# The loads and splits of the weights carry the highest priority of the scheduler

## The chip, the core and the metric

The kernel runs on one core of a Trainium2 chip. The metric is the device time of one execution in microseconds (us); the time before is the median of three runs. A profiled execution is a further run, and what is read from the trace belongs to that one alone.

The engines have these names in the rows: PE is TensorE (matrix products; PEld its weight loads), DVE is VectorE, ACT is ScalarE, POOL is GpSimd, SP is SyncE, which here issues DMA transfers only. Each engine works through its own list of instructions.

## The reference

Two blocks in sequence, everything in float32. x and ctx are 256 x 2048 each.

```python
for l in range(2):                                   # first block
    shift, scale, gate = split(silu(c) @ w_ada[l] + b_ada[l], 3)         # and the same for c_ctx
    h  = rms(x, norm_w[l]) * (1 + scale) + shift     # hc from ctx in the same way
    qa, ka, va, qb, kb, vb, qc, kc, vc, z = project_stream(h, w_in[l], ...)
    o = three kinds of attention (8, 12 and 6 heads) on queries of h, keys of h and hc
    x = x + gate * ((o * silu(z)) @ w_out[l])        # and ctx, in the first layer only
h = rmsnorm(x, pre_norm_mix)                         # second block
x = x + rmsnorm(token_mixer(h, w_in_2, ...), ...)    # spatial gating and gated linear attention
x = x + rmsnorm(memory_cross_attention(...), ...)
x = x + rmsnorm(conv_ffn(rmsnorm(x, ...), ffn_w_up, ..., ffn_w_down), ...)
```

What takes the time are the dense products with large weights: w_in (2048 x 6208, twice), w_out, w_in_2 (2048 x 12304), the projections of the mixer, and the feed-forward weights (2048 x 11264 and 5632 x 2048).

## The kernel before

**Products.** A float32 product is made of three products in a faster format, float32r. Each operand is split into hi (the value rounded to float32r) and lo (the rest), and the kernel adds hi by hi, hi by lo and lo by hi. `split` (L418) does this with one copy on ACT (L420) and one subtraction on DVE (L421). Activations are split once and kept; weights are split as they stream in.

**The weight stream.** `order()` lists all pairs of weight tiles (two times 128 x up to 512 values, 512 KB) in the order of their use, 894 pairs in all. `load` (L441) takes a buffer of the tag raw, of which there are three, and issues the transfer on SP (L448). `run_ahead` (L451) takes one tile of a loaded pair, a buffer each of the tags hi and lo (four of each), and splits. `weights` (L433) hands a pair to a product. In the text of the program a split stands about two tiles ahead of its use.

**Dense loops.** `dense` (L462) has activations as stationary operand and adds up one PSUM bank for each column group of 128 tokens: four groups for most products of the first block, two elsewhere. `denseT` (L488) has weights as the stationary operand. Both use the tag d, of which there are four banks. After the last k-tile the caller's evac empties the banks on ACT, DVE or both.

**Everything else.** Norms, attention and gates are cut into small stages (`push`, `urge`, `defer`) that `tick` (L368) calls between matrix products, by a clock of estimated TensorE time. So the text of the program already interleaves dense work with attention.

**adaLN.** For the first layer, `ada_pe` (L668) computes shift and scale on PE, from 256 KB loads on SP (L689, L694), in five parts; each part of h is usable when its part is there. The other shifts, scales and gates come from `ada_steps` (L718): loads on SP (L736) and a product with a running sum on DVE (L739), strewn over the first block.

**What sets the order.** The kernel is written for a scheduler that receives all instructions in one block, each with a priority that is its place in the text. It goes through the block with a model of the engines' times. Whenever an engine is free in that model, it takes, among the instructions whose inputs and buffers are there, the one of the lowest number. The order that comes out is fixed for each engine, with semaphores where one engine needs another. On the chip every engine keeps to that order, whatever the real times are.

**The start.** `block1` (L1408) issues the sixteen loads of x and ctx (L1441) in turn with the sixteen first adaLN loads (L689), squares and sums each row of tokens on ACT (L515), and makes h through transposes, DVE (L540) and ACT (L543). The first products (`first_products`, L1382) need h.

Of the kernel before, what the change touches and what calls it, by code (L numbers as in the profile page):

```python
# [235 lines left out]
class K:  # L236
# [204 lines left out]
    def load(self):  # L441

        if self.order_at < len(self.order):
            name, k0, pieces = self.order[self.order_at]
            self.order_at += 1
            raw = self.str.tile([128, 2, 512], F32, name=self.name("raw"), tag="raw", bufs=3)
            n, src = self.w(name).block(k0, pieces)
            self.nc.sync.dma_start(raw[:, :, :n], src)  # L448
            self.loaded += [raw[:, j, :n] for j in range(2)]

    def run_ahead(self):  # L451

        if not self.loaded:
            self.load()
        if self.loaded and len(self.whole) < 2:
            raw = self.loaded.pop(0)
            n = raw.shape[-1]
            hi, lo = (self.str.tile([128, 512], F32R, name=self.name(x), tag=x, bufs=4) for x in ("hi", "lo"))
            self.split(hi[:, :n], lo[:, :n], raw)
            self.whole.append((hi, lo))  # L460

    def dense(self, act, kts, w, pieces, cols, evac, what="d", skip={}):  # L462
# [177 lines left out]
class Block1(K):  # L640
# [266 lines left out]
    def layer(self, l, h, hl, hcols, qcols, x_get, x_put):  # L907
# [161 lines left out]
        def job_ab(g, m, s):  # L1069
# [56 lines left out]
            for hd in (2 * m, 2 * m + 1):  # L1126
                for q in range(2):
                    st = [lambda hd=hd, q=q: load(hd, q), self.ahead] if g == "a" and s == 0 else []
                    st += [lambda hd=hd, q=q: prepare(hd, q), self.padding, lambda hd=hd, q=q: first(hd, q), self.soft, lambda hd=hd, q=q: part(hd, q), self.lag, lambda hd=hd, q=q: second(hd, q)]
                    self.push(*st, *([self.lag2, end] if hd % 2 and q else []))  # L1130
# [886 lines left out]
```

## Time and profile before

| | us |
|---|---|
| median of three runs | 3467.62 (3465.45 to 3474.96) |
| profiled execution | 3477.03 |
| its span, from first to last instruction | 3475.3 |
| TensorE busy in the span | 3353.6 |
| VectorE busy | 2298.3 |
| ScalarE busy | 1788.2 |
| mean granted TensorE clock | 0.985 of 2.4 GHz |

A row of a timeline has the start and the length in us, the engine, the line of the program, the operation, what is written and read, and how many instructions were merged; in brackets stands the idle time of the engine just before, and what ended it. A row of a list of waits has the engine and line that waited, what ended the wait, the total in us, how many times, and the longest. A row of stretches has, for each engine, busy time and instructions, then the granted clock (1.00 is 2.4 GHz, 0.50 is 1.2 GHz), the busy share of the DMA engines and GB/s.

### The profile page before, as it was taken

What the parts mean: (1) busy time and instruction counts of PE and PEld (TensorE: products, weight loads), DVE (VectorE), ACT (ScalarE), POOL (GpSimd) and SP (SyncE); (2) the same over time, 40 slices, a digit from 0 to 9 for tenths busy, and PEclk for the clock granted to TensorE, in tenths of its full rate; (3) what the DMA queues carried; (4) which work ended last, traced back from release to release, by engine and by line L of the source; (5) the groups of instructions that cost most, each with busy time, mean ns of one, the idle gap of its engine ahead of it and who ended that gap; (6) DMA issues with size and microseconds to landing.
All of it is one profiled execution on the core that took longest, in us unless ns stands there. A gap on an engine that the chain in (4) does not pass through costs nothing. (4 is left out here: it accounts for less than half of the span.)

```text
span 3475.3 us, 54483 instructions
## 1 busy us (share of the span) xinstructions
PE 3353.6 (96%) x19530; PEld 2879.6 (83%) x19530; DVE 2298.3 (66%) x4939; ACT 1788.2 (51%) x3556; POOL 315.7 (9%) x472
## 2 busy tenths in 40 slices
PE   7999999999999999999999999999999899999998
PEld 4577778788787888887777999888788899999886
DVE  3488988778866576887664555555666766666554
ACT  3345655346435365765474445545556555555544
POOL 0022210103120121111200000000000000000000
PEclk9999999999999999999999999999999999999999
DMA  8845444642565544444544535555655455555554
GB/s 295 290 118 153 130 146 144 207 131 86 172 210 158 162 113 139 143 153 139 176 145 158 183 116 182 192 190 190 205 177 168 146 182 183 182 187 196 189 194 164
DMA packets 226767, 590.28 MB, mean 170 GB/s; under 512 B 39904, under 2 KB 63184, under 8 KB 226496
## 3 DMA queue, kind: packets, MB, share of 16 engines
q1 hardware_dynamic: 221104, 570.41, 51.1%
q0 software_dynamic: 4864, 15.69, 1.5%
q8 instruction: 153, 2.51, 0.3%
q14 instruction: 118, 0.97, 0.1%
q10 hardware_dynamic: 528, 0.71, 0.1%
HBM read 582.48 MB, written 4.24 MB: 169 GB/s over the span
## 5 line engine op out<-in xcount | busy, mean ns | idle before, releaser
L421 DVE TENSOR_TENSOR lo<-raw,hi 128x512 fp32r<-128x512 f32 (+3 forms) x1788 | 1206.7, 679 | 846.2 <-ACT hi L420 838.7
L420 ACT ACTIVATE hi<-raw 128x512 fp32r<-128x512 f32 (+3 forms) x1788 | 1090.4, 614 | 1238.0 <-DVE lo L421 271.1
L502 PE MATMUL upd<-hi,hi 128*128 128x256 f32 x1408 | 399.2, 284 | 0.0
L504 PE MATMUL upd<-lo,hi 128*128 128x256 f32 x1408 | 399.1, 283 | 0.0
L505 PE MATMUL upd<-hi,lo 128*128 128x256 f32 x1408 | 398.8, 283 | 0.0
L739 DVE SCALAR_TENSOR_TENSOR scr<-raw,cb 128x512 f32<-128x512 f32 x448 | 299.1, 693 | 35.8 <-DMA raw<-in_w_ada_dram 17.8
L504 PEld LDWEIGHTS upd<-lo,hi 128*128 128x128 f32 x1408 | 270.8, 192 | 0.3 <-DVE lo L546 0.3
L505 PEld LDWEIGHTS upd<-hi,lo 128*128 128x128 f32 x1408 | 270.8, 192 | 0.0
L502 PEld LDWEIGHTS upd<-hi,hi 128*128 128x128 f32 x1408 | 270.7, 192 | 0.0
L399 POOL TENSOR_TENSOR sm<-sm,mhalf 128x2 f32<-128x2 f32 (+4 forms) x116 | 117.0, 1010 | 1406.2 <-DVE sm L398 1400.9
L481 PE MATMUL downd<-hi,hi 128*128 128x512 f32 x352 | 137.7, 391 | 0.0
L483 PE MATMUL downd<-hi,lo 128*128 128x512 f32 x352 | 137.7, 391 | 0.0
L482 PE MATMUL downd<-lo,hi 128*128 128x512 f32 x352 | 137.6, 391 | 0.0
L602 ACT ACTIVATE P<-Ss,sm 128x512 f32<-128x512 f32 (+1 forms) x164 | 99.5, 608 | 67.7 <-DVE sm L598 49.6
L408 ACT ACTIVATE PT<-pTt 128x256 f32<-128x256 f32 x226 | 79.3, 381 | 64.9 <-PE pTt L619 55.0
L481 PE MATMUL L0outd<-hi,hi 128*128 128x512 f32 x256 | 101.2, 395 | 4.3 <-DVE ot L1361 3.0
L505 PE MATMUL L0zd<-hi,lo 128*128 128x512 f32 x256 | 100.4, 392 | 2.4 <-DVE lo L421 2.4
L598 DVE TENSOR_REDUCE sm<-Ss 128x1 f32<-128x512 f32 (+1 forms) x164 | 95.1, 585 | 8.9 <-PE Ss L591 7.9
L502 PE MATMUL L0zd<-hi,hi 128*128 128x512 f32 x256 | 100.4, 392 | 0.4 <-DVE kpe L414 0.4
L482 PE MATMUL L0outd<-lo,hi 128*128 128x512 f32 x256 | 100.1, 391 | 0.0
L483 PE MATMUL L0outd<-hi,lo 128*128 128x512 f32 x256 | 99.8, 392 | 0.3 <-DVE lo L421 0.3
L504 PE MATMUL L0zd<-lo,hi 128*128 128x512 f32 x256 | 100.0, 391 | 0.0
(570 smaller groups left out, 8451.3 us busy)
## 6 DMA issues: line engine op xcount, KB each, us to landing
raw<-in_w_in_dram SPq DMA_DIRECT2D x344, 512.0 KB, 3.6
raw<-in_w_ada_dram SPq DMA_DIRECT2D x384, 256.0 KB, 3.5
raw<-in_ffn_w_up_dram SPq DMA_DIRECT2D x176, 512.0 KB, 3.3
raw<-in_w_out_dram SPq DMA_DIRECT2D x104, 512.0 KB, 3.6
raw<-in_ffn_w_down_dram SPq DMA_DIRECT2D x88, 512.0 KB, 3.2
raw<-in_w_proj_b_dram SPq DMA_DIRECT2D x32, 512.0 KB, 3.3
raw<-in_w_in_dram SPq DMA_DIRECT2D x32, 288.0 KB, 3.3
raw<-in_w_proj_a_dram SPq DMA_DIRECT2D x16, 512.0 KB, 4.0
```

Of the source, the lines that this page charges most:

```text
L399: nc.gpsimd.tensor_tensor(r, ms, self.mhalf[:, :n], op=OP.pow)
L420: self.nc.scalar.activation(hi, src, AF.Copy)
L421: self.nc.vector.tensor_sub(lo, src, hi.bitcast(F32))
L481: nc.tensor.matmul(ps[t][:, a], lhsT=xh, rhs=hi[:, a], start=first, stop=False)
L482: nc.tensor.matmul(ps[t][:, a], lhsT=xh, rhs=lo[:, a], start=False, stop=False)
L483: nc.tensor.matmul(ps[t][:, a], lhsT=xl, rhs=hi[:, a], start=False, stop=last)
L502: nc.tensor.matmul(p, lhsT=hi[:, s], rhs=xh, start=kt == 0 and c % per == 0, stop=False, skip_group_check=True)
L504: nc.tensor.matmul(p, lhsT=hi[:, s], rhs=xl, start=False, stop=False, skip_group_check=True)
L505: nc.tensor.matmul(p, lhsT=lo[:, s], rhs=xh, start=False, stop=kt == nk - 1, skip_group_check=True)
L598: nc.vector.tensor_reduce(nm[:, 0:1], S[:, :nk], op=OP.max, axis=AX.X, negate=True)
L602: nc.scalar.activation(P[:, :nk], S[:, :nk], AF.Exp, bias=nm[:, 0:1], accum_out=nm[:, 1:2])
L739: nc.vector.scalar_tensor_tensor(self.temp("scr"), raw, 1.0, st[s], op0=OP.mult, op1=OP.mult, accum_out=st["p"][:, s, k, q:q + 1])
```

## The change

The issue of each weight load, and both instructions of each weight split, are written inside `high_priority()`. This context gives what is written in it the priority numbers from zero on, as if it stood at the start of the program, and goes back to the former count on its exit. No instruction is added, removed or changed in shape, and the numbers of buffers stay as they are. Splits of activations (`halves`, `unit`) keep their priority.

```diff
@@ -445,7 +445,8 @@
             self.order_at += 1
             raw = self.str.tile([128, 2, 512], F32, name=self.name("raw"), tag="raw", bufs=3)
             n, src = self.w(name).block(k0, pieces)
-            self.nc.sync.dma_start(raw[:, :, :n], src)
+            with self.tc.high_priority():
+                self.nc.sync.dma_start(raw[:, :, :n], src)
             self.loaded += [raw[:, j, :n] for j in range(2)]
 
     def run_ahead(self):
@@ -456,7 +457,8 @@
             raw = self.loaded.pop(0)
             n = raw.shape[-1]
             hi, lo = (self.str.tile([128, 512], F32R, name=self.name(x), tag=x, bufs=4) for x in ("hi", "lo"))
-            self.split(hi[:, :n], lo[:, :n], raw)
+            with self.tc.high_priority():
+                self.split(hi[:, :n], lo[:, :n], raw)
             self.whole.append((hi, lo))
```

## Rows read from the trace of the kernel before

**Rows 1.** The page's first part: busy time, share of the span, instructions.
```profile
PE 3353.6 (96%) x19530; PEld 2879.6 (83%) x19530; DVE 2298.3 (66%) x4939; ACT 1788.2 (51%) x3556; POOL 315.7 (9%) x472
```

**Rows 2.** Stretches: the start up to the first product, and the up projection.
```profile
0.00:36.00 36.00, 16.10 (x91) 6.87 (x91) 7.09 (x37) 16.46 (x43) 8.68 (x31) 1.00 0.97 345
2708.00:3219.00 511.00, 511.00 (x4247) 510.70 (x4246) 339.75 (x582) 286.35 (x486) 2.18 (x4) 1.00 0.55 182
```

**Rows 3.** Waits of PE: on splits of weights, and one on an eviction.
```profile
PE L1qbd L481 <- ACT hi L420: 5.1, 1, 5.1
PE mbd L481 <- ACT hi L420: 3.1, 1, 3.1
PE xkd L505 <- DVE lo L421: 3.1, 1, 3.1
PE vsd L481 <- ACT hi L420: 2.9, 2, 2.6
...
PE L0zd L505 <- DVE lo L421: 2.4, 3, 1.3
...
PE L0cqd L482 <- DVE lo L421: 2.2, 1, 2.2
...
PE L1qbd L482 <- DVE lo L421: 1.8, 4, 1.1
...
PE L0vbd L481 <- DVE a L1403: 1.6, 3, 0.9
```

**Rows 4.** Stretches behind five waits, PE alone: busy (x), clock, DMA, GB/s.
```profile
499.90:503.30 3.40, 3.40 (x12) 0.50 0.82 242
1356.40:1363.50 7.10, 5.95 (x17) 0.50 0.43 142
1769.60:1773.00 3.40, 3.37 (x15) 0.51 0.57 167
2452.50:2455.70 3.20, 3.20 (x7) 0.50 0.59 205
2592.30:2595.70 3.40, 3.40 (x18) 0.50 0.72 224
```

**Rows 5.** Timeline of the start, up to the first dense product.
```profile
1.35 0.70 POOL L775 DMA_DIRECT2D rows<-in_rows_dram  x1 [0.34 <-issue]
...
24.44 1.01 SPq L448 DMA_DIRECT2D raw<-in_w_in_dram  x2
...
27.21 0.63 ACT L515 ACTIVATE scr<-x 128x512 f32<-128x512 f32 x1 [1.31 <-DMA x<-in_ctx_dram]
...
35.94 0.78 PE L481 MATMUL L0firstd<-hi,hi 128*128 128x512 f32 x1
```

**Rows 6.** Timeline of DVE before the wait of L0cqd.
```profile
496.67 0.68 DVE L739 SCALAR_TENSOR_TENSOR scr<-raw,cb 128x512 f32<-128x512 f32 x1
...
497.88 1.28 DVE L421 TENSOR_TENSOR lo<-raw,hi 128x512 fp32r<-128x512 f32 x2
```

**Rows 7.** Timeline of DVE before the wait of xkd.
```profile
2586.34 4.77 DVE L1522 SCALAR_TENSOR_TENSOR x<-y,sm,x 128x512 f32<-128x512 f32 x4 [0.44 <-POOL sm L399]
```

**Rows 8.** Timeline of ACT before the wait of vsd.
```profile
1766.98 0.63 ACT L1591 ACTIVATE e<-e 128x512 f32<-128x512 f32 x1
```

**Rows 9.** Timeline of ACT in the product L1qbd.
```profile
1340.04 0.94 ACT L420 ACTIVATE hi<-raw 128x384 fp32r<-128x384 f32 x2 [2.08 <-DMA raw<-in_w_in_dram]
```

**Rows 10.** Timeline of ACT before the wait of mbd.
```profile
2451.19 0.63 ACT L515 ACTIVATE scr<-mem 128x512 f32<-128x512 f32 x1 [4.18 <-DMA mem<-in_mem_dram]
...
2451.82 0.61 ACT L420 ACTIVATE hi<-raw 128x512 fp32r<-128x512 f32 x1
```

**Rows 11.** Timeline of DVE where L0firstd ends and L0vbd begins.
```profile
219.55 0.68 DVE L421 TENSOR_TENSOR lo<-raw,hi 128x512 fp32r<-128x512 f32 x1
...
220.15 1.28 DVE L1403 TENSOR_TENSOR a<-a,L0firstd 128x512 f32<-128x512 f32 x2
```

**Rows 12.** Waits of ACT: its longest on slots of one product of layer 0.
```profile
ACT hi L420 <- PE L0zd L504: 98.4, 51, 2.7
```

## The prediction

> **What bounds the kernel now.** I read the page first: TensorE is busy for 3353.6 us of a span of 3475.3 us [rows 1]. So at most the remaining 122 us, and whatever TensorE does at a slow clock, can be won by any reordering. Next I cut the span into stretches: in the 511 us of the up projection, TensorE is busy for all 511 us [rows 2]. There the splits already keep up, and another order can win nothing. Third, I listed what TensorE waits for [rows 3]. The reader is to look for two names there: "ACT hi L420" and "DVE lo L421" are the two halves of a split, and a dense product (L481 to L483, L502 to L505) that waits for one of them lacks a weight. These rows add up to 5.1 + 3.1 + 3.1 + 2.9 + 2.4 + 2.2 + 1.8 = 20.6 us. Fourth, I asked for the granted clock just after the five longest of those waits [rows 4]. It stands at 0.50 (1.2 GHz) for 3.4, 7.1, 3.4, 3.2 and 3.4 us, where it is 2.4 GHz in steady work. Half of each such stretch is lost: 1.7 + 3.5 + 1.7 + 1.6 + 1.7 = 10.2 us. A late split therefore costs 20.6 + 10.2 = 30.8 us in all, which is the whole prize of the change.
>
> **Does the scheduler do what the edit asks?** The trace shows that it hoists what is ready as far as it can: the load of "rows" belongs to rope_tables, which the code calls behind the whole first product, and yet GpSimd issues it at 1.35 us [rows 5]. An instruction at priority zero is therefore taken the moment that its buffer is free and its data is there. What stays the limit is buffers: three for raw, four each for hi and lo. No split can go further ahead than these allow, and the amount of work on every engine stays the same. Only orders change: of ACT and DVE (1788 splits on each), and of SP (894 loads).
>
> **Part 1, splits on DVE and ACT: a gain.** Before L0cqd's wait of 2.2 us, DVE runs adaLN products (L739), and only then two lo halves [rows 6]. What L739 makes is a gate that the output product is the first to use, so nothing is lost by taking the lo first. The same order makes L0zd wait (2.4 us), and before xkd's wait DVE does four steps of the residual update, 4.77 us, and then the lo [rows 7]. I take these three whole: 2.2 + 2.4 + 3.1 us of waits and 1.7 + 1.7 us of slow clock, 11.1 us. The wait of vsd (2.9 us, and 1.7 us of clock) has ACT busy with logarithms and exponentials (L1586, L1591) in front of a split [rows 8]: whole, 4.6 us. L1qbd (5.1 + 1.8 us, and 3.5 us of clock, 10.4 us) I take at two thirds, 6.9 us: in that stage ACT also waits for the raw load itself, 2.08 us at one place [rows 9], and no priority helps against that. mbd (3.1 us, and 1.6 us of clock, 4.7 us) I take at half, 2.4 us: there ACT stands at a Square that waits 4.18 us for the memory input, and the split behind it starts right when the Square ends [rows 10]. If the scheduler believes that the input has landed earlier than it does, it will again put the Square first. Sum: 11.1 + 4.6 + 6.9 + 2.4 = 25.0 us saved. The bounds are 11.1 us (only the DVE places) and 30.8 us (all of it).
>
> **Part 2, loads on SP: a loss at the start.** Before, the first raw load is issued at 24.44 us, behind all sixteen loads of x and ctx and the sixteen first adaLN loads on the same queue [rows 5]. At priority zero it is ready at time zero, since its buffers are empty. Three raw loads of 512 KB fill the three buffers. Their splits need only themselves, and two tiles of four halves go through at once (four slots), which frees two more raw buffers. So five loads, 5 x 524 KB = 2.62 MB, go ahead of nearly all of x. The start is bound by transfer: 345 GB/s and a DMA share of 0.97 in the first 36 us [rows 2], so five loads put the last x back by 2.62 MB / 345 GB/s = 7.6 us, and three by 4.6 us. All of it is on the path: the last Square of ctx starts at 27.21 us because it waited for its load, and the first dense product follows at 35.94 us through a chain of norm, adaLN and transposes that contains no weight [rows 5]. Nothing is paid back, as TensorE does not run short of weights later in that stage. I take 7.6 us lost, with bounds 4.6 and 7.6 us. A gain is excluded, since the first product waits for h and not for a weight. Later on the same queue the raw loads also pass adaLN loads, bias loads and gates. Each is put back by an issue of about half a us (two took 1.01 us [rows 5]), and all of them are asked for well ahead of their use by the text, so I take nothing for that; without that cover it would be half a us for each that PE waits for.
>
> **Part 3, what the splits push back: a loss at changes of product.** In layer 0 a product of four column groups fills all four banks that dense work has. The next product needs the last bank nine matmuls after the change, and nine of 512 columns at 2.4 GHz are 1.9 us. An eviction of about 0.7 us fits into that with one split of 0.68 us ahead of it, and with two it does not. The trace has one such place: at 219.55 us a lo half goes ahead of the additions that empty the banks, and TensorE then waits for "a L1403" three times [rows 11], 1.6 us in total [rows 3]. The code has 43 changes with all four banks in use (34 in layer 0, 9 in layer 1). In such stages a slot falls free only once in a k-tile of four column groups, so two ready splits are rare. I take one change in ten, 4 x 1.6 = 6.4 us lost, with bounds 0 and twice that, 12.8 us. In the second block a product uses two of the four banks, so an eviction has a whole product's time, and this costs nothing there. Attention's softmax steps are also pushed back, by at most the few splits that the slots allow, and dense work covers them on TensorE, so I take nothing; where no dense work is left, it would be 0.68 us for each such split.
>
> **Sum.** 25.0 us saved, 7.6 + 6.4 = 14.0 us lost: 11.0 us less. The profiled execution took 3477.0 us (span 3475.3 us and 1.7 us around it), 9.4 us above the median of 3467.6 us, so the forecast is 3466 us for such an execution and 3467.6 - 11.0 = 3456.6 us for the median; I write 3456. About 0.3% (10.4 us) is what a measurement of this kernel can tell from no change, and the forecast lies just past it. Its own range is 3441 (30.8 us saved, 4.6 us lost, no bank waited for) to 3477 (11.1 us saved, 7.6 + 12.8 us lost).
>
> **Rivals.** *The waits move on.* The wait for a split goes, but what was ahead of it is then late: k stacks behind L1qbd, exponentials behind vsd, and TensorE waits there instead. Half of the gain stays, 12.5 us, against 14.0 us lost: 1.5 us more, 3469 us. For it: TensorE's list has dozens of small waits of other kinds. Against it: most of them have dense work ready to fill the place.
>
> *Evictions held in the queue, slower.* The place is the change of product in layers 0 and 1, and the price is the 1.6 us of the one that the trace shows. ACT already stands at the head of its queue for a slot: 51 times, 98.4 us in all, for L0zd alone [rows 12]. A split put early then holds what is behind it. If 20 of the 43 changes pay, that is 32 us: 25.0 saved, 7.6 + 32 lost, 14.6 us more, 3482 us. It decides from about 11 changes on, where 17.4 us eat the net gain of 25.0 - 7.6. Against it: only one of the 43 shows the cost now, although lo halves stand among evictions in many places. The Trainium skill, "Perfetto Trace Analysis", section "Tensor Engine Instruction (MATMUL, LD_WEIGHTS)", says that the queues of ACT, DVE and GpSimd are strictly first in, first out, so an early split that isn't ready stops all behind it. By that rule this rival is the natural outcome. The trace agrees as far as the order goes: the ready split behind the waiting Square started only after it [rows 10].
>
> *The order hardly changes.* If splits are ready just when nothing else is, as in the second block, only the start moves: 7.6 us more, 3475 us. Against it: DVE's order before L0cqd shows a case where both were ready [rows 6].
>
> **Chances.** The forecast 0.44; the waits move on 0.27; evictions held 0.19; order unchanged 0.10. The second and the fourth lie within 0.3%. So faster 0.44, same 0.37, slower 0.19. For eight in ten I take 3440 to 3484: it holds the forecast's range, both middle cases and about half of the slow one.
>
> **What would show it.** Right: the first dense product starts at about 43 us; raw loads are SP's first issues; the rows of L0cqd, L0zd and xkd that wait for L421 are gone, and with them the half clock at 500 and 2592 us; the up projection takes 511 us still. Wrong: the first product starts where it did (loads not hoisted); waits for "a L1403", "ot L1361" or other evictions grow past 13 us; L1qbd waits for DMA instead; or new stretches of half clock behind attention's steps.

## The result, and the profile after

The kernel became slower. The median went from 3469.6 to 3503.7 us, a ratio of 1.0092 with a 95% interval of 1.0078 to 1.0105, about 32 us (the two medians as they stand are 34 us apart, the figure that the expectations use). The forecast was 3456 us, with 3440 to 3484 as its range; both the sign and the range were wrong. The profiled execution of the changed kernel took 3503.4 us, with a span of 3501.6 us against 3475.3 us: 26.3 us more. In the changed kernel's rows the lines of `dense` and `denseT` are two higher than before (L481 is now L483, L505 is L507), and up to two higher in the runs below; the split stays at L420 and L421.

The page's first part of the kernel after, the line that answers to [rows 1]:

```profile
PE 3365.2 (96%) x19530; PEld 2878.7 (82%) x19530; DVE 2304.3 (66%) x4939; ACT 1792.7 (51%) x3556; POOL 319.5 (9%) x472
```

The same instructions run, but TensorE is busy for 11.6 us more and idle for 14.7 us more (136.4 against 121.7 us). The next view is that of stretches, as in [rows 2]: the start and the up projection after.

```profile
0.00:47.00 47.00, 18.15 (x106) 7.18 (x107) 9.22 (x40) 18.37 (x46) 10.53 (x31) 1.00 0.92 308
2734.00:3245.00 511.00, 510.94 (x4240) 509.94 (x4239) 342.83 (x580) 288.83 (x485) 2.18 (x4) 1.00 0.54 182
```

The up projection is as it was. The start now takes 47 us instead of 36, and at a lower rate of transfer: 308 GB/s over the stretch instead of 345. The waits of TensorE after come first below, and the rows of the same kinds before in the second fence:

```profile
PE adao L700 <- DMA raw<-in_w_ada_dram: 29.6, 9, 19.2
...
PE sts L851 <- DVE kl L874: 5.0, 3, 3.5
PE trs L532 <- DVE sm L398: 3.6, 1, 3.6
...
PE Ss L593 <- DVE kl L872: 3.0, 3, 2.2
...
PE pTt L621 <- DVE P L614: 2.9, 5, 1.1
PE L0zd L507 <- DVE lo L421: 2.7, 1, 2.7
...
PE sts L851 <- POOL ro L806: 2.6, 2, 2.2
PE vsd L483 <- ACT hi L420: 2.6, 3, 0.9
PE L0vbd L483 <- DVE a L1405: 2.2, 3, 1.0
PE sts L851 <- DVE q L874: 1.8, 1, 1.8
...
PE mbd L483 <- ACT hi L420: 1.2, 1, 1.2
...
PE L1qbd L483 <- ACT hi L420: 0.4, 1, 0.4
...
PE xkd L507 <- DVE lo L421: 0.2, 1, 0.2
```

```profile
PE adao L698 <- DMA raw<-in_w_ada_dram: 13.0, 7, 8.9
...
PE trs L530 <- DVE sm L398: 2.4, 1, 2.4
...
PE sts L849 <- DVE kl L872: 2.3, 3, 1.5
...
PE Ss L591 <- DVE kl L870: 1.9, 1, 1.9
...
PE pTt L619 <- DVE P L612: 0.8, 2, 0.5
...
PE sts L847 <- DVE q L872: 0.2, 1, 0.2
```

Three things are to be seen. The change does what it says: the waits for splits of [rows 3] shrink from 20.6 us to about 8 us, and L0cqd's is gone. Against them stand longer or new ones, the largest of them on steps of attention and rope (kl, P, q, ro) and on one of a norm (sm). These six kinds grew by 2.7 + 1.1 + 2.1 + 1.6 + 2.6 + 1.2 = 11.3 us (ro has no row before); smaller kinds grew and shrank beside them. And the products of adaLN wait 16.6 us longer for their own loads.

Read along the groups of dense products, the loss comes in two parts. The first dense product starts 11.1 us later and L0vbd, the first group behind the first products, 17.4 us later (238.36 us instead of 220.98). Between there and the end another 9 us come, in many pieces, with gains in between that don't last.

### The profile page after: what moved, and what is told of

It is laid out like the page before. It is cut to its first block, busy times and chain, and to the rows that moved or that the text cites. A ratio compares the mean times of both kernels' runs of the same rounds, so it can differ in the third digit from the quotient of the medians.

```text
span 3501.6 us, 54518 instructions
## 1 busy us (share of the span) xinstructions
PE 3365.2 (96%) x19530; PEld 2878.7 (82%) x19530; DVE 2304.3 (66%) x4939; ACT 1792.7 (51%) x3556; POOL 319.5 (9%) x472
## 4 chain that ended last, share of the span: by engine, by line
PE 58%; issue 12%; DVE 6%; ACT 2%; DMA 1%; POOL 1%; POOLq 0%; DVEq 0%; ACTq 0%; SPq 0%
PE upd L506 5%; PE upd L507 5%; PE upd L504 5%; PE downd L485 2%; PE downd L483 2%; PE downd L484 2%; DVE lo L421 2%; PE L0outd L483 1%; PE oo L636 1%; PE L0outd L485 1%; PE L0outd L484 1%; PE Ss L593 1%; PE wo2d L484 1%; PE wo2d L483 1%; PE wo2d L485 1%
## 5 line engine op out<-in xcount | busy, mean ns | idle before, releaser
L421 DVE TENSOR_TENSOR lo<-raw,hi 128x512 fp32r<-128x512 f32 (+3 forms) x1788 | 1207.2, 679 | 856.5 <-ACT hi L420 845.4
L420 ACT ACTIVATE hi<-raw 128x512 fp32r<-128x512 f32 (+3 forms) x1788 | 1091.5, 614 | 1271.1 <-DVE lo L421 268.1
L507 PE MATMUL upd<-hi,lo 128*128 128x256 f32 x1408 | 398.9, 283 | 0.0
L507 PEld LDWEIGHTS upd<-hi,lo 128*128 128x128 f32 x1408 | 270.9, 192 | 0.0
L483 PE MATMUL downd<-hi,hi 128*128 128x512 f32 x352 | 137.7, 391 | 0.0
L483 PE MATMUL L0outd<-hi,hi 128*128 128x512 f32 x256 | 101.1, 395 | 4.3 <-DVE ot L1363 2.9
L507 PE MATMUL L0zd<-hi,lo 128*128 128x512 f32 x256 | 100.6, 394 | 2.7 <-DVE lo L421 2.7
```

The costliest lines, as they stand in the source:

```text
L420: self.nc.scalar.activation(hi, src, AF.Copy)
L421: self.nc.vector.tensor_sub(lo, src, hi.bitcast(F32))
L483: nc.tensor.matmul(ps[t][:, a], lhsT=xh, rhs=hi[:, a], start=first, stop=False)
L507: nc.tensor.matmul(p, lhsT=lo[:, s], rhs=xh, start=False, stop=kt == nk - 1, skip_group_check=True)
```

## The experiments

All ratios are to the kernel before, on the same chip, with 95% intervals; 0.1% is 3.5 us. In each diff the lines are those of `load` or `run_ahead`, and `order_at` is the number of the pair in the order of use. The first products use pairs 1 to 24, the rest of the first layer pairs 25 to 159, the second layer 160 to 318, and the second block 319 to 894.

### Loads against splits, early against late

```
e1_loads:   with self.tc.high_priority():                                   # load only
e2_splits:  with self.tc.high_priority():                                   # split only
e3_late:    with self.tc.high_priority() if self.order_at > 24 else ...     # load and split
e4_early:   with self.tc.high_priority() if self.order_at <= 24 else ...    # load and split
```

> Only the weight loads carry the priority; the splits keep their place in the text. Theory L (the loss is made on SP: raw loads stand ahead of x and of adaLN loads, at the start and in the first stage): first dense product at about 47 us as in the changed kernel, waits of adaLN products for their loads well above the 13 us of before, time 17 to 30 us above before. Theory Q (the loss is made in the queues of ACT and DVE, where splits stand ahead of other work): only the start costs, 8 to 11 us above before, and the rest of the loss of 34 us is gone.

> Only the splits carry the priority; the loads keep their place in the text. Theory L: the first dense product starts at about 36 us as before, the waits of L0cqd, L0zd and xkd for the lo half are gone, time 0 to 11 us below before. Theory Q: 15 to 25 us above before, with longer waits for evictions and attention's steps.

> Loads and splits carry the priority from the 25th pair of weight tiles on, that is behind the pairs of the first products. Theory L: start and first stage as before; what is left is the rest, which by the starts of the dense groups was about 9 us between 220 us and the end: 5 to 10 us above before. Theory Q: the 17 us of start and first stage are not all from there, and 15 to 25 us above before are left.

> Loads and splits carry the priority for the first 24 pairs alone, those of the first products. Theory L: L0vbd starts about 17 us later than before and nothing is paid back: 17 to 25 us above before, and together with the kernel that has the other pairs it adds up to the loss of the whole change, 34 us. Theory Q: 8 to 11 us above before, the start alone.

Measured: e1_loads 1.0045 (1.0031 to 1.0058), e2_splits 1.0049 (1.0036 to 1.0062), e3_late 1.0043 (1.0031 to 1.0056), e4_early 1.0046 (1.0031 to 1.0061). Each is about 15 us slower, and either pair adds up to the loss of the whole. So both theories hold, each for one half, though the loads alone stay just under theory L's 17 to 30 us. With the loads alone, the first dense product starts 11.0 us late and L0vbd 15.2 us late, and the rest of the kernel just follows: the last product starts 13.6 us late. With loads and splits raised from pair 25 on (e3_late), the first dense product starts as before and L0vbd 1.8 us late, and the loss collects from the second group of z to the end of the second layer. That the splits would cost nothing, as theory L had it, fell; so did theory Q's view that loads cost at the start only.

The two halves lose their time in different places. These are the first parts of the pages of e1_loads (span 3489.0 us) and e2_splits (span 3486.1 us):

```profile
PE 3351.7 (96%) x19530; PEld 2878.4 (82%) x19530; DVE 2300.5 (66%) x4939; ACT 1788.0 (51%) x3556; POOL 319.1 (9%) x472
PE 3365.1 (97%) x19530; PEld 2882.0 (83%) x19530; DVE 2304.0 (66%) x4939; ACT 1792.4 (51%) x3556; POOL 318.1 (9%) x472
```

With the loads alone TensorE is busy about as long as before (3353.6 us) and idle for 137.3 us instead of 121.7: that half is waiting. With the splits alone it is idle for 121.0 us, as before, and busy for 11.5 us more, at a mean granted clock of 0.987 (0.985 before). So the new waits only take the place of those that went, and what is lost is TensorE's own time for the same instructions. e3_late has most of its loss there too (3367.7 us busy, 125.4 us idle). Each profile is a single execution, but all ten in which no split behind pair 24 is raised lie between 3346.4 and 3360.3 us busy, and the changed kernel, e2_splits, e3_late, e13_lo and e14_off40 between 3361.5 and 3367.7 us.

### The start and the first stage

```
e5_three:   ... if self.order_at <= 3 else ...          # load and split
e10_five:   ... if self.order_at <= 5 else ...
e9_mid:     ... if 4 <= self.order_at <= 24 else ...
```

> Only the first three pairs carry the priority, so SP has three weight loads ahead of x and none that waits for a buffer. Theory T (the start is lost to transfer alone, bytes over 345 GB/s): the first dense product is 4.6 us later than before, the fourth and fifth load cost the other 3.0 us of five, and the 9.5 to 11 us of the runs with five need another reason. Theory S (SP stands at the fourth load until a buffer is free, with x behind it): three loads give 4 to 6 us and the rest of the 11, 5 to 7 us, is the standing; and the first stage behind it loses nothing, as its loads are where they were before. Time 4 to 7 us above before in both; 10 or more would say that the place of the first load, not the buffers, matters.

> Loads and splits of the first five pairs alone carry the priority. With three, the first dense product was 6.1 us later, and the first stage behind it 5.2 us shorter. Theory S: first dense product 9.5 to 11 us later than before, and since only three loads' worth of that is paid back, L0vbd 5 us later or more, time 5 to 10 us above before. Theory A: the first stage pays back all of it as with three, L0vbd within 2 us of before, time within 4 us of before, and the loss of 14 us of the first 24 pairs comes from pairs 6 to 24.

> Loads and splits of pairs 4 to 24 carry the priority; the first three stay behind x and the first adaLN loads. Theory A (in the first stage raw loads ahead of adaLN loads cost by themselves): the first dense product at 36 us as before, L0vbd 4 to 8 us later than before, time 4 to 8 us above before. Theory S (what costs is the fourth and fifth load at the start, where SP stands with x behind it): first dense product and L0vbd within 2 us of before, time within 3 us of before.

Measured: e5_three 1.0007 (0.9998 to 1.0017), e10_five 1.0007 (0.9998 to 1.0016), e9_mid 1.0020 (1.0009 to 1.0031). The rows are PE's timelines, the first dense product and the first of L0vbd, for e5_three, e10_five and e9_mid in this order:

```profile
42.07 0.48 PE L483 MATMUL L0firstd<-hi,hi 128*128 128x512 f32 x1
221.87 0.47 PE L483 MATMUL L0vbd<-hi,hi 128*128 128x512 f32 x1 [0.95 <-DVE a L1405]
```

```profile
46.42 0.78 PE L483 MATMUL L0firstd<-hi,hi 128*128 128x512 f32 x1
227.98 0.47 PE L483 MATMUL L0vbd<-hi,hi 128*128 128x512 f32 x1 [0.95 <-DVE a L1405]
```

```profile
36.72 0.78 PE L483 MATMUL L0firstd<-hi,hi 128*128 128x512 f32 x1
232.93 0.47 PE L483 MATMUL L0vbd<-hi,hi 128*128 128x512 f32 x1 [0.98 <-DVE a L1405]
```

Before, these stand at 35.94 and 220.98 us. Three loads ahead of x put the first product back by 6.1 us, but the stage behind it is 5.2 us shorter, so almost all is paid back. It comes back as TensorE's own time, 172.4 instead of 177.0 us in the stage: 15 of its products are done before the first dense one, and its granted clock is 1.00 instead of 0.99. Its waits for adaLN loads in the stage are not shorter (6.3 against 3.6 us). Five loads put it back by 10.5 us, and 3.5 us come back. Raw loads within the stage (e9_mid) leave the start alone and make the stage 11.2 us longer. TensorE's waits for adaLN loads between the first dense product and L0vbd, before, in the changed kernel and in e9_mid:

```profile
PE adao L698 <- DMA raw<-in_w_ada_dram: 3.6, 5, 1.8
PE adao L700 <- DMA raw<-in_w_ada_dram: 10.4, 8, 2.3
PE adao L700 <- DMA raw<-in_w_ada_dram: 12.2, 8, 2.1
```

Theory A is right for that stage, where 8.6 of the 11.2 us are these waits; L0vbd is even 11.9 us late, more than its 4 to 8. Theory S is right in that the fourth and fifth load cost at the start and are not paid back, but five loads cost 2.4 us (-0.7 to 5.6), less than its 5 to 10. The times agree in order, three or five 2.4 us, pairs 4 to 24 7.0 us; the sum of the parts, 9.4 us, is below the 16 us of e4_early, though the intervals are wide enough for both.

A part of what five loads cost beyond their bytes is in the changed kernel's SP queue: its timeline at the start, and in the second fence the longest of its waits for a buffer up to 40 us.

```profile
0.81 1.34 SPq L449 DMA_DIRECT2D raw<-in_w_in_dram  x3
2.19 4.08 SPq L1443 DMA_DIRECT2D x<-in_x_dram  x2
11.09 1.53 SPq L449 DMA_DIRECT2D raw<-in_w_in_dram  x2
12.67 0.90 SPq L691 DMA_DIRECT2D raw<-in_w_ada_dram  x2
```

```profile
SPq L449 <- DVE lo L421: 5.5, 2, 4.7
```

The fourth load stands at the head of SP's queue until a lo half has freed its raw buffer, 4.7 us, and behind it stand the adaLN loads and the rest of x. Before, the first adaLN load was issued at 1.72 us, now at 12.67 us. But this stand is a small part of the 10.5 us. From three to five loads the first dense product moves by 4.4 us, and the bytes of two loads at 345 GB/s are 3.0 us, which leaves at most 1.4 us for it. Three loads, none of which waits for a buffer, already cost 6.1 us where their bytes give 4.6; no run shows where the other 1.5 us come from.

### The splits by stage

```
e6_layer0:  with self.tc.high_priority() if 24 < self.order_at <= 159 else ...     # split only
e7_layer1:  with self.tc.high_priority() if 159 < self.order_at <= 318 else ...
e8_block2:  with self.tc.high_priority() if self.order_at > 318 else ...
```

> Only the splits of pairs 25 to 159 (first layer, behind the first products) carry the priority. Theory O (raised splits give TensorE another order of products, with more changes between dense work and attention steps, and each change costs): 5 to 8 us above before, spread over all groups from the second group of z on, without one long wait. Theory P (the prediction: the waits of L0cqd and L0zd for the lo half go, a few evictions wait): 6 us below to 2 us above before.

> Only the splits of pairs 160 to 318 (second layer) carry the priority. Theory G (given back: the dense products of that stage get early, but attention ends the stage): L1zd starts about 10 us earlier than before, counted from the start of the layer, the first L1qcd does not, and the time is 1 to 5 us above before. Theory P (the prediction): the 10 us stay, time 7 to 10 us below before.

> Only the splits from pair 319 on (the second block) carry the priority. Theory G (given back: xq and xv start 4 to 6 us earlier, the up projection does not, since a chain of attention and norm ends that stage): within 3 us of before. Theory P (the prediction: vsd 4.6, mbd 2.4 and xkd 4.8 us saved): 10 to 12 us below before.

Measured: e6_layer0 1.0019 (1.0009 to 1.0029), e7_layer1 1.0013 (1.0004 to 1.0021), e8_block2 1.0002 (0.9994 to 1.0011): 6.6, 4.5 and 0.7 us, 11.8 us together, which agrees with e2_splits and e3_late within their intervals. The forecast for these parts had gains of up to 6, of 7 to 10 and of 10 to 12 us; there is none anywhere. The times are those of theories O and G.

The second layer shows best why. In e7_layer1's trace the L1qbd waits are down to 0.5 and 0.3 us, and counted against before, the next products start early by 9 us (L1cqd) and 15 us (L1zd). The first L1qcd is then only 1.5 us ahead of where it would have been. These are PE's waits in that stretch, and in the second fence the stretch before and in e7_layer1, from the first L1qbd to the first L1qcd, for PE alone:

```profile
PE sts L850 <- POOL ro L805: 2.7, 2, 2.3
PE sts L850 <- DVE q L873: 1.8, 1, 1.8
...
PE L1qbd L482 <- ACT hi L420: 0.5, 1, 0.5
```

```profile
1326.90:1483.90 157.00, 146.39 (x946) 0.97 0.49 148
1326.20:1481.70 155.50, 148.76 (x946) 1.00 0.50 149
```

Instead of 5.1 + 1.8 us for splits [rows 3], TensorE waits 2.7 + 1.8 us for rope's sum and for q: steps that VectorE and GpSimd reach later. All idle time of the stretch together still shrinks, from 10.6 to 6.7 us, and the half clock behind the old wait is gone. What takes most of this away is TensorE's own time: the same 946 products take 148.8 us instead of 146.4. If the 5.95 us at half clock [rows 4] are counted half, they took an estimated 143.4 us before, 5.4 us less. By the order of its instructions in the two traces, TensorE changes 105 times between a dense product and another one in this stretch, and 83 times before. That these changes are the cost is likely, but no run shows it by itself.

### TensorE's order held fixed

```
# run_ahead: splits of pairs 25 to 894 at the highest priority, and at the end of the program:
mm = [i for i in tc.nc.cur_bb.bb.instructions if type(i).__name__ == "InstMatmult"]
same = [mm[a + j] for a, n in RUNS for j in range(n)]      # RUNS: TensorE's order in the kernel before
for p, i in zip(same, same[1:]):
    tc.add_manual_dep(i, p.name, edge, reason="same_order")
```

> The splits of pairs 25 to 894 carry the priority, and every matrix product is tied behind the one that stands before it in the kernel before, so that TensorE's order is that of before while the orders of ScalarE and VectorE change (712 and 1890 places differ). With TensorE's order free the same splits cost 12 to 15 us. Theory O (the loss is TensorE's new order, with more changes between dense products and attention steps): 0 to 10 us below before. Theory Q (the loss is what splits hold up on ScalarE and VectorE): 8 to 15 us above before, with waits for evictions or attention steps that before did not have.

Measured: 1.0177 (1.0164 to 1.0190), 62 us slower. The gain that theory O expected of the old order isn't there: with it the same splits cost four times as much. The first part of its page (span 3531.7 us), and PE's waits in it:

```profile
PE 3360.3 (95%) x19530; PEld 2879.6 (82%) x19530; DVE 2311.3 (65%) x4939; ACT 1792.2 (51%) x3556; POOL 317.6 (9%) x472
```

```profile
PE pTt L620 <- DVE P L613: 11.0, 13, 1.8
...
PE sts L850 <- POOL ro L805: 8.1, 2, 7.0
PE sts L850 <- DVE kl L873: 6.9, 3, 4.2
```

P is a step of the softmax, kl and ro belong to attention's operands and rope. With the order held, TensorE is idle for 171.4 us, 50 us more than in e2_splits, and busy for 3360.3 instead of 3365.1 us, at a lower mean clock (0.983). So with raised splits and the order held, attention's steps come late; with the order free, TensorE's own time grows instead. This run therefore doesn't clear the new order, theory O's suspect, of the 15 us; it shows only that keeping the old one is dearer. How much of the 62 us comes from holding the order at all is open, since no run holds it with the splits where they were.

### Which engine, and how far

```
e12_hi:     high_priority() on the ACT copy alone,        pairs 25 to 894
e13_lo:     high_priority() on the DVE subtraction alone, pairs 25 to 894
e14_off40:  high_priority(offset=40)  on both halves,     pairs 25 to 894
e15_low15:  high_priority(offset=-15) on both halves,     pairs 25 to 894
e15_low40:  high_priority(offset=-40) on both halves,     pairs 25 to 894
```

> Only the hi halves (the copy on ScalarE) of pairs 25 to 894 carry the priority. Theory D (what is pushed back are attention's steps on VectorE, the busier of the two engines, 66% against 51%): within 3 us of before, as the lo halves stay where they were. Theory E (both engines alike): 5 to 9 us above before, about half of the 14 us of both halves.

> Only the lo halves (the subtraction on VectorE) of pairs 25 to 894 carry the priority. Theory D: 10 to 15 us above before, as much as with both halves, with the waits for kl, P and the rope of before grown. Theory E: 5 to 9 us above before.

> The splits of pairs 25 to 894 stand 40 places earlier in priority than in the text, instead of at the highest. If the loss goes with how far attention's steps are pushed back: 0 to 8 us above before. If any raise past the neighbouring steps costs the whole: 11 to 15 us above before. If the short raise is enough for the late weights and pushes nothing far back: 3 to 8 us below before.

> The splits of pairs 25 to 894 stand 15 places later in priority than in the text, so that attention's steps go ahead of them. If attention's steps are what ends the stages of the first block, and splits have slack: 0 to 6 us below before. If the splits of before have no slack: the waits for hi and lo grow, 5 us or more above before.

> The splits of pairs 25 to 894 stand 40 places later in priority than in the text. If the splits of before have slack and attention's steps do not: within 4 us of before, as with 15 places, or a little below. If 40 places are more than the four buffers of hi and lo cover: the waits for hi and lo grow, 5 us or more above before.

Measured: e12_hi 1.0019 (1.0010 to 1.0028), e13_lo 1.0055 (1.0042 to 1.0069), e14_off40 1.0027 (1.0015 to 1.0039), e15_low15 1.0000 (0.9988 to 1.0013), e15_low40 1.0032 (1.0020 to 1.0045). The lo halves on VectorE are the costly ones, 19 us, more than either theory gave; the hi halves alone cost 6.6 us, more than theory D's 3 us and within theory E's 5 to 9. A raise by 40 places already costs 9 us. A lowering by 15 places costs nothing that shows (-4.2 to 4.5 us), and one by 40 places 11 us. There the splits are late, as PE's waits in e15_low40 show against the 2.2 and 1.8 us of [rows 3]:

```profile
PE L1qbd L483 <- DVE lo L421: 5.3, 4, 2.9
PE L0cqd L483 <- DVE lo L421: 4.1, 1, 4.1
```

### Raising or lowering other work instead

```
e16_softmax:  with self.tc.high_priority(offset=40):     # maximum, exponential, reciprocal, division
e17_side40:   with self.tc.high_priority(offset=-40):    # the adaLN side products, L739
```

> The softmax steps (maximum, exponential, reciprocal, division) of every attention stand 40 places earlier in priority; loads and splits are as before. If these steps are what TensorE lacks when splits go first, the waits for P shrink and the time is 0 to 8 us below before. If any change of order near the splits costs: 5 us or more above before, with the waits for hi and lo grown.

> Loads and splits are as before; the adaLN side products on VectorE stand 40 places later in priority than in the text. If they are what stands ahead of late splits and attention steps: L0cqd's and L0zd's waits for lo go, no wait for kl takes their place, and the time is 2 to 8 us below before. If VectorE is simply full in the first layer, so that any order makes something late: within 4 us of before. If the side products then hold up the output product or their own loads: 5 us or more above before.

Measured: e16_softmax 1.0021 (1.0012 to 1.0030), e17_side40 1.0028 (1.0019 to 1.0037). Neither gives a faster kernel. Raised softmax steps cost 7 us, so the loss can't be put down to them alone. The side products were suspected because of what stands on VectorE in the changed kernel at L0cqd. The rows are DVE's timeline ahead of the wait (with further side products and earlier steps of kl left out), then PE's timeline at the wait, then the stretch behind it for PE alone (busy, clock, DMA share, GB/s):

```profile
519.79 0.68 DVE L421 TENSOR_TENSOR lo<-raw,hi 128x512 fp32r<-128x512 f32 x1
...
522.41 0.68 DVE L741 SCALAR_TENSOR_TENSOR scr<-raw,cb 128x512 f32<-128x512 f32 x1
...
523.75 0.67 DVE L421 TENSOR_TENSOR lo<-raw,hi 128x512 fp32r<-128x512 f32 x1
...
524.78 0.48 DVE L874 SCALAR_TENSOR_TENSOR kl<-sts,vt,k 64x256 fp32r<-64x256 f32 x1
```

```profile
525.41 0.41 PE L851 MATMUL sts<-ident,ro 128*128 128x128 f32 x2 [3.52 <-DVE kl L874]
```

```profile
525.80:529.20 3.40, 3.40 (x11) 0.50 0.12 22
```

Here is the change in small. Before, VectorE did side products and then a lo half, and TensorE waited 2.2 us for the lo [rows 3, 6]. Now the lo halves pass, kl is what comes behind the side products, and TensorE waits 3.52 us for kl. The stretch of half clock that followed the old wait (0.50, 1.2 GHz) [rows 4] follows the new one too. VectorE has little room there: in the 380 us from 240 us on (before) and from 256 us on (after) it is busy for 337.6 and 337.8 us, the third figure after the length being its own:

```profile
240.00:620.00 380.00, 369.49 (x2007) 293.34 (x2006) 337.62 (x1026) 217.16 (x564) 72.26 (x121) 0.99 0.49 145
```

```profile
256.00:636.00 380.00, 368.13 (x2004) 289.70 (x2003) 337.78 (x1017) 217.04 (x562) 74.94 (x120) 1.00 0.48 144
```

Lowering the side products should then have freed splits and kl alike. It did not: e17_side40 is 9.7 us slower than before, and its waits for kl and q are longer than those of the changed kernel (5.0 and 1.8 us). PE's waits in e17_side40:

```profile
PE sts L851 <- DVE kl L874: 6.3, 3, 4.4
...
PE sts L849 <- DVE q L874: 4.0, 1, 4.0
```

What remains is a finding without one culprit. Splits moved by 40 places or more, up or down, on one engine or both, and softmax steps or side products moved by 40: with TensorE's order free, every such run that reaches both layers costs between 6.6 and 19 us. Only 15 places did no harm. That the late steps are those of attention and rope is shown by the waits, that VectorE's half alone costs no less than both is shown by e13_lo, and that with the splits alone the loss stands in TensorE's busy time and not in its waits is shown by the page of e2_splits. Why the same products take longer in the new order, which of VectorE's steps would have to go first, and whether any order beats that of the text, is open.

## Why the prediction was wrong, point by point

**What bounds the kernel: right as far as it went.** The up projection held nothing to win, and the prize was the 20.6 us of waits and 10.2 us of slow clock. What the list of waits didn't say is that VectorE has 42 us of idle time in 380 in the first layer, so that a step put forward can put another back.

**Does the scheduler do what the edit asks: right.** Three raw loads are SP's first issues, and the waits of L0cqd, L1qbd and xkd are gone or nearly so; L0zd has one of 2.7 us instead of three of 2.4 us in all.

**Part 1, 25.0 us saved: the step that failed.** The waits did shrink, by about 12 us, and the half clock at 2592 us has gone. But "nothing is lost by taking the lo first" was argued from what the side product makes (a gate that is used late) and not from what else stood in VectorE's queue. Six kinds of waits for other steps grew by 11.3 us, and the half clock at 500 us came back behind kl. And "the amount of work on every engine stays the same. Only orders change" named the orders of ACT, DVE and SP and put TensorE's own at nothing: with the splits alone its waits come to the same sum as before (121.0 against 121.7 us) and its busy time grows by 11.5 us. Taken by stage, the gain of 25.0 us measured as a loss of 6.6 us in the first layer and 4.5 us in the second, and 0.7 us (-2.1 to 3.8) in the second block, where vsd, mbd and xkd were to bring 11.8 us.

**Part 2, 7.6 us lost at the start: too small, in two terms.** The five loads were right, and their bytes too. The first product was 11.1 us late, not 7.6. Of the 3.5 us more, 1.5 come with the first three loads (6.1 instead of 4.6) and stay unexplained; at most 1.4 come with SP's stand at the fourth load, with x behind it. The step went through the buffers and saw that the fourth load needs one freed, but costed only bytes. "Nothing is paid back" was wrong as well: three loads cost 6.1 us at the start and came back to 0.9 us at L0vbd. The other term was put at nothing: "the raw loads also pass adaLN loads ... all of them are asked for well ahead". From the first dense product to L0vbd the stage took 6.3 us longer than before, and with raw loads raised in it alone 11.2 us, while TensorE's waits for adaLN loads there went from 3.6 to 10.4 and 12.2 us. The cover named in the text, loads asked for well ahead, was used up in the first stage: TensorE waited 13.0 us for adaLN loads up to L0vbd before the change already, 3.6 us of it behind the first dense product, a row of the list of waits that the prediction passed over.

**Part 3, evictions 6.4 us, attention nothing: the wrong way round.** L0vbd's wait for the additions went from 1.6 to 2.2 us and no other eviction grew, so evictions cost about half a us. Attention's steps were put at nothing because dense work would cover them. They did become late, and the cover isn't free: where TensorE's order could change, the waits came out even and its busy time grew; where it couldn't (e11_same_order), the loss was 62 us instead of 15.

**The rivals.** The mechanism of "the waits move on" came true: behind L1qbd, where it named k stacks, TensorE waits for rope's sum and q. With the splits alone it took all that was won in waits, not half, and the loss beyond that is in TensorE's busy time, which no rival named. "Evictions held in the queue" had the right kind of cost, a split ahead of other work in an in-order queue, but put it on evictions, whose waits hardly grew. The Trainium skill, "Perfetto Trace Analysis", section "Tensor Engine Instruction (MATMUL, LD_WEIGHTS)", has the queues of ACT, DVE and GpSimd strictly in order; the trace agrees, as kl starts only behind the lo halves put ahead of it (524.78 us behind 523.75), but what such a queue holds up had to be read from the rows of each stage. Neither rival was given the first stage's adaLN loads, and so none reached 3504 us; the range left out a case in which both the start and the queues lose.

**The signs.** Right: raw loads first on SP, L0cqd's row gone and xkd's down to 0.2 us, half clock at 2592 us gone, up projection 511 us. The first product came at 47, not 43 us. The signs of failure that were named (evictions past 13 us, L1qbd waiting for DMA) didn't come; the last one, new half clock behind attention's steps, did.

## What to carry to other kernels

Raising the priority of one kind of work in an in-order queue is a swap: cost it by naming what stands behind it on that engine in the same 10 us, not by the wait that it removes. Then read the busy time of the busiest engine beside its waits, since another order of the same instructions can lengthen it. Before calling a load early, look at the head of its queue, since a load that waits for a buffer holds every load behind it. And a stage in which an engine is 90% busy has an order worth keeping; measure a small move (here 15 places) before a large one.

## What the runs showed that was not expected

The price of the same raised splits was 15 us with TensorE's order free and 62 us with it held. With the order free (e2_splits) the waits came out even and TensorE's busy time grew by 11.5 us with the same instructions, though the mean granted clock went from 0.985 to 0.987; with the order held TensorE waited 50 us more. The loads, in contrast, cost waits alone: 137.3 us idle in e1_loads instead of 121.7. And raising the lo half of a split alone cost no less than raising both halves: 19 us against 15, with intervals that overlap.
